# A hybrid encoder block on one NeuronCore: the input normalised ahead of its first products, decays summed by one scan per head pair

## The chip, the cores and the metric

The kernel runs on one NeuronCore of a Trainium2 chip. The metric is the device time of one execution in microseconds, lower is better; the median of several runs is compared.

## What is computed

One residual block over 512 tokens of width 1024, all in float32. The parts that matter here:

```python
h = rmsnorm(x, attn_norm_g)                     # x * rsqrt(mean(x*x) + eps) * g
proj = h @ w_in
p_sb, p_rw, p_gate = jnp.split(proj, [SB_COLS, SB_COLS + RW_COLS], axis=-1)
...
xs = token_shift(p_rw, rwkv_shift_mu)           # p + (prev - p) * mu
r, k, v, w_lo, a_lo, g_lo = jnp.split(xs, offs, axis=-1)
w_log = -jax.nn.softplus(-(decay_base + jnp.tanh(w_lo) @ decay_up)) - 0.5
decay = jnp.exp(-jnp.exp(w_log))
...
y = rwkv7_recurrence(rh, wh, kh, vh, -kk, kk * ah)
...
gates = jax.nn.sigmoid(p_gate.reshape(...) + branch_gate_b)
x = x + jnp.sum(gates * up, axis=2) @ w_out
h2 = rmsnorm(x, ffn_norm_g)
u_gate, u_val = jnp.split(causal_depthwise_conv(h2 @ w_ffn_up, ...), 2, axis=-1)
x = x + (jax.nn.silu(u_gate) * u_val) @ w_ffn_down
```

Two branches use the projection: a stick-breaking attention (8 heads) and an RWKV-7 recurrence (8 heads). The recurrence is computed in chunks of 64 tokens, and needs, in each chunk, the sum of the log decays from a token to the chunk's end.

## The kernel before

Everything is held transposed: channels on the 128 partitions, the 512 tokens along the row. A float32 product is made of three: each operand is split into a rounded high part and the rest, and high by high, high by low and low by high are summed in PSUM (`mm1`, L124). Weights come in blocks of 128 columns (`load_w`, L99): one load on SyncE's queue into `wraw`, a cast to `whi` on ScalarE, two subtractions that give the halves of `wlo` (L116), on GpSimd in the middle part of the program and on VectorE elsewhere. `wraw` and `whi` have two buffers, `wlo` three. One block of the projection is 24 products of 512 columns.

The head (L197 to L285) loads x in eight slices `xt`, scales each by the gain alone, splits it into `hhi` and `hlo`, and multiplies slices as they arrive with the first weight block w0 (the low-rank inputs of decay and iclr, bank `pl0`). The squares are summed on the side; one product with a matrix of -1 (L254) sums them over channels, and two ScalarE steps make `rs`, one factor for each token. The second block w1 (the first k of the recurrence, bank `pk0`) follows. Since the factor is missing in the products, every evacuation of a projection block multiplies by `rs` on VectorE: `evac_rw` (L362, tile u), `evac_at` (L371, tiles rawq, rawk, vT), `evac_gl` (L380, L383), `evac_gate` (L803, tile gs), and L965 late in the program.

The middle part runs three kinds of streams interleaved: four head pairs of the recurrence (`rw_stream`), four of the attention (`att_stream`), and `dense_stream`, which makes the remaining projection blocks one after the other in two PSUM banks `pd`. `interleave` (L881) orders TensorE's work by a table of latencies LAT; a scheduler orders the other engines. In `rw_stream`, the low-rank products (L410, L412) give the log decays s, a scan for each of the eight chunks sums them from the chunk's end (L425), L427 takes s off again, sll and slh (L438, L121) feed the sums over a head, and later, a solve of 31 short steps on VectorE (L538, L540) follows on transfers `sc` and `N` through DRAM. Thirteen of sixteen gate blocks are made in this part and parked in DRAM, three are made later (L962 to L966). Then come the branch products, `w_out` and the feed-forward part, with products back to back.

Of the kernel before, what the change touches and what calls it, by code (L numbers as in the profile page):

```python
# [8 lines left out]
F32 = mybir.dt.float32  # L9
F32R = mybir.dt.float32r  # L10
# [6 lines left out]
P = 128  # L17
# [35 lines left out]
def hybrid_block(ctx: ExitStack, tc: tile.TileContext, xT, w_in, vecs, decay_up, iclr_up, out_gate_up,  # L53
# [24 lines left out]
    def f(ap):  # L78
        return ap.bitcast(F32)
# [31 lines left out]
    def load_w2(w, nk=KT):  # L111
        hi, los, raw = w
        k0 = 4 * len(los)
        n = min(4, nk - k0)
        lo = wpool.tile([P, 4, P], F32R, tag="wlo", name="wlo", bufs=3)
        (G if state.get("pool") else V).tensor_tensor(lo[:, 0:n], raw[:, k0 : k0 + n], f(hi[:, k0 : k0 + n]),  # L116
                                                      op=ALU.subtract)
        los.append(lo)
# [16 lines left out]
    def bank(pool=None, tag="pd"):  # L135
        return (pool or psd).tile([P, T], F32, tag=tag, name=tag)
# [47 lines left out]
    U1 = cpool.tile([P, NC, CH // 2], F32, name="U1")  # L184

    RW0 = SBC
    LR0 = RW0 + 3 * BW
    rs = keep.tile([P, T], F32, tag="rs", name="rs")  # L190
    ph1 = ExitStack()
    psr = ph1.enter_context(tc.tile_pool(name="psr", bufs=3, space=PSUM))
    psz = ph1.enter_context(tc.tile_pool(name="psz", bufs=2, space=PSUM))
# [1 line left out]
    with tc.tile_pool(name="p0", bufs=1) as p0, \  # L195
# [8 lines left out]
        def wdma(w, c0, k0, k1):  # L204
            nc.sync.dma_start(w[2][:, k0:k1], w_in[k0 * P : k1 * P, c0 : c0 + P].rearrange("(k p) c -> p k c", p=P))

        w0, w1 = wtiles(), wtiles()
        A.dma_start(vec, vecs[:, 0:NVEC1])
        nc.sync.dma_start(xt[:, 0:1], xv[:, 0:1])
        wdma(w0, LR0, 0, 4)  # L210
        nc.sync.dma_start(xt[:, 1:2], xv[:, 1:2])
        wdma(w0, LR0, 4, 8)
        for k in range(2, KT, 2):
            nc.sync.dma_start(xt[:, k : k + 2], xv[:, k : k + 2])
        wdma(w1, RW0 + BW, 0, 8)
        lraw = [p0.tile([P, BW], F32, name=f"lraw{j}") for j in range(2)]
        for j, src in enumerate((decay_up, iclr_up)):
# [2 lines left out]
        tmpc = p0.tile([P, P], F32, name="tmpc")  # L220
        V.memset(tmpc, -1.0)
        V.tensor_copy(none_, tmpc)
        pl0, pn, pk0 = bank(psr, "pr"), bank(psr, "pr"), bank()
        sq = []
        for k in range(KT):
            if True:
                if k % 4 == 0:
                    A.copy(w0[0][:, k : k + 4], w0[2][:, k : k + 4])
                    load_w2(w0)
                act(hhi[:, k], xt[:, k], AF.Identity, scale=vcol("ag", k))  # L230
                V.scalar_tensor_tensor(hlo[:, k], xt[:, k], vcol("ag", k), f(hhi[:, k]),
                                       op0=ALU.mult, op1=ALU.subtract)
                mm1(pl0, w0, k, h_acts[k], k == 0, k == KT - 1)

                sq.append(p0.tile([P, T], F32, name=f"sq{k}"))
                if k in (0, 3):
                    G.tensor_tensor(sq[k], xt[:, k], xt[:, k], op=ALU.mult)
                else:
                    act(sq[k], xt[:, k], AF.Square)
                if 0 < k < 4:  # L240
                    G.tensor_tensor(sq[0], sq[0], sq[k], op=ALU.add)
                elif k > 4:
                    V.tensor_tensor(sq[4], sq[4], sq[k], op=ALU.add)
            if k == KT - 1:
                V.tensor_tensor(sq[0], sq[0], sq[4], op=ALU.add)
                state["pool"] = True
                for h in range(2):
                    A.copy(w1[0][:, 4 * h : 4 * h + 4], w1[2][:, 4 * h : 4 * h + 4])
                    load_w2(w1)
        for k in range(KT):  # L250
            for part in range(2):
                PE.matmul(pk0, w1[0][:, k], h_acts[k][part], start=(k + part == 0), stop=False)
            if k == 1:
                PE.matmul(pn, f(none_), sq[0], start=True, stop=True)  # L254
        for k in range(KT):
            PE.matmul(pk0, w1[1][k // 4][:, k % 4], hhi[:, k], start=False, stop=(k == KT - 1))
# [5 lines left out]
        V.tensor_scalar(ka1, vcol("keya", 0, 4), -1.0, 1.0, op0=ALU.mult, op1=ALU.add)  # L262
        qg8 = cpool.tile([P, 1], F32, name="qg8")
        V.tensor_scalar(qg8, vcol("qg"), 0.125, None, op0=ALU.mult)
        act(rs, pn, AF.Ln, scale=-1.0 / D, bias=eps_n)
        act(rs, rs, AF.Exp, scale=-0.5)
        wfirst = load_w(w_in[:, RW0 : RW0 + P], KT)
        V.tensor_tensor(sq[1], pl0, rs, op=ALU.mult)
        wal = p0.tile([P, T], F32, name="wal")
        shift_evac(wal, sq[1], 12)  # L270
        load_set(SET_SG, (AF.Sigmoid, AF.Tanh))
        act(wal[0:64], wal[0:64], AF.Tanh)
        for j in range(2):
# [15 lines left out]
        ntri = cpool.tile([P, P], F32R, name="ntri")  # L289
        idb = cpool.tile([P, P], BF16, name="idb")  # L290
        mskb = cpool.tile([P, P], BF16, name="mskb")
        one = cpool.tile([P, CH], F32, name="one")
        eps_g = cpool.tile([P, 1], F32, name="eps_g")
        V.memset(eps_g, GN_EPS)
        G.memset(ident, 0.0)
# [62 lines left out]
    AD = [dict() for _ in range(4)]  # L358

    def evac_rw(p, which, ps):  # L360
        u = rwp.tile([P, T], F32, tag="u", name="u")
        V.tensor_tensor(u, ps, rs, op=ALU.mult)  # L362
        RD[p][which] = rwp.tile([P, T], F32, tag="x" + which, name="x" + which)
        shift_evac(RD[p][which], u, 4 * "rkv".index(which) + p)

    def evac_at(p, which, ps):
        if which == "v":
            t_ = atp.tile([P, T], F32, tag="e", name="vT", bufs=3)
        else:
            t_ = atp.tile([P, T], F32, tag="raw" + which, name="raw" + which)  # L370
        V.tensor_tensor(t_, ps, rs, op=ALU.mult)  # L371
        AD[p][which] = t_

    def evac_gl(g, ps):

        u = rwp.tile([P, T], F32, tag="u", name="u")
        n = 32 if g is gl1 else P
        g_ = u[0:n]
        if n == P:
            V.tensor_tensor(g_, ps, rs, op=ALU.mult)  # L380
        else:
            A.copy(g_, ps[n : 2 * n])
            V.tensor_tensor(g_, g_, ps[0:n], op=ALU.add)  # L383
            V.tensor_tensor(g_, g_, rs[0:n], op=ALU.mult)
        y = atp.tile([P, T], F32, tag="gs", name="gy")[0:n]
        shift_evac(y, g_, 13 if n == P else 14, slice(0, n))
        act(g_, y, AF.Abs)
        act(g_, g_, AF.Exp, scale=-1.0)
        act(g_, g_, AF.Ln, bias=1.0)
        V.scalar_tensor_tensor(y, y, 0.0, g_, op0=ALU.min, op1=ALU.subtract)  # L390
        if n == P:
            his, lo = gl0[0:1], gl0[1]
        else:
            his, lo = (gl1[0:32], gl1[32:64]), gl1[64:96]
        for hi in his:
            act(hi, y, AF.Exp)
        act(g_, y, AF.Exp)
        V.tensor_tensor(lo, g_, f(his[0]), op=ALU.subtract)

    def rw_stream(p):  # L400
# [20 lines left out]
        s, ic = sic  # L421

        c = tmp(0)
        for ch in range(NC):
            V.tensor_tensor_scan(c3(c)[:, ch, ::-1], one, c3(s)[:, ch, ::-1], 0.0, op0=ALU.mult, op1=ALU.add)  # L425
        fx = tmp(1)
        V.tensor_tensor(fx, c, s, op=ALU.subtract)  # L427
        GC = rwp.tile([P, NC, 1], F32, tag="GC", name="GC", bufs=3)
# [371 lines left out]

    def evac_gate(c, b, ps):
        g = atp.tile([P, T], F32, tag="gs", name="gs", bufs=1)
        V.tensor_tensor(g, ps, rs, op=ALU.mult)  # L803
        gd = gdram.tile([P, T], F32, name=f"gd{c}_{b}")
        A.dma_start(gd, g)
        gates[c, b] = gd
# [148 lines left out]
    for c in sorted(range(KT), key=lambda c: (c, 0) in gates):  # L955
        terms = []
        for b in range(2):
            g = p2.tile([P, T], F32, tag="g", name="g", bufs=5)
            if (c, b) in gates:
                nc.sync.dma_start(g, gates[c, b])  # L960
            else:
                w = load_w(w_in[:, GOFF + b * D + c * P : GOFF + b * D + (c + 1) * P], KT)  # L962
                pg = bank(psf, "pf")
                mm3(pg, w, h_acts)
                V.tensor_tensor(g, pg, rs, op=ALU.mult)  # L965
            act(g, g, AF.Sigmoid, bias=vcol("bg", b * KT + c))  # L966
# [115 lines left out]
```

## Time and profile before

| | before |
|---|---|
| median of 3 runs | 920.23 us (919.76 to 923.12) |
| profiled execution | 921.83 us, span of its instructions 920.1 us |
| TensorE busy | 873.9 us (95% of the span) |
| VectorE busy | 625.9 us (68%) |
| ScalarE busy | 455.8 us (50%) |
| GpSimd busy | 200.2 us (22%) |
| mean granted clock of TensorE | 0.977 |

A busy TensorE is not one at its peak: its products overlap each other in the records, and they last longer at a low clock. The busy shares are means over stages that differ, so the profile is read by stretches. In the rows, PE is TensorE, PEld its weight load, DVE VectorE, ACT ScalarE, POOL GpSimd, SP SyncE; L12 is line 12 of the kernel; tile names are the program's.

### The profile page before, as it was taken

What the parts mean: (1) busy time and instruction counts of PE and PEld (TensorE: products, weight loads), DVE (VectorE), ACT (ScalarE), POOL (GpSimd) and SP (SyncE); (2) the same over time, 40 slices, a digit from 0 to 9 for tenths busy, and PEclk for the clock granted to TensorE, in tenths of its full rate; (3) what the DMA queues carried; (4) which work ended last, traced back from release to release, by engine and by line L of the source; (5) the groups of instructions that cost most, each with busy time, mean ns of one, the idle gap of its engine ahead of it and who ended that gap; (6) DMA issues with size and microseconds to landing.
All of it is one profiled execution on the core that took longest, in us unless ns stands there. A gap on an engine that the chain in (4) does not pass through costs nothing.

```text
span 920.1 us, 12850 instructions
## 1 busy us (share of the span) xinstructions
PE 873.9 (95%) x4716; PEld 675.8 (73%) x4716; DVE 625.9 (68%) x1160; ACT 455.8 (50%) x791; POOL 200.2 (22%) x219
## 2 busy tenths in 40 slices
PE   6979887898999999999999999999999999999998
PEld 3757665666767766777777888888888888888886
DVE  7585898898799679365766656777777777632322
ACT  5846665653764666358654445444444444311111
POOL 6552455326525443424000000000000000000000
PEclk9995998998999999999999999999999999999999
DMA  6320313313303331622555443333333333333331
GB/s 188 109 62 13 86 46 64 87 46 79 102 28 75 84 83 36 154 59 59 195 167 155 139 126 91 104 103 92 92 99 107 92 92 93 105 105 118 106 114 46
DMA packets 164479, 87.54 MB, mean 95 GB/s; under 512 B 28384, under 2 KB 155488, under 8 KB 164416
## 3 DMA queue, kind: packets, MB, share of 16 engines
q1 hardware_dynamic: 161392, 81.61, 31.5%
q10 hardware_dynamic: 3024, 5.11, 1.5%
q8 instruction: 37, 0.61, 0.3%
q14 instruction: 26, 0.21, 0.1%
HBM read 78.31 MB, written 8.39 MB: 94 GB/s over the span
## 4 chain that ended last, share of the span: by engine, by line
PE 71%; DVE 17%; ACT 5%; issue 3%; DMA 3%; POOL 0%; SPq 0%; ACTq 0%; DVEq 0%; POOLq 0%
PE pf L129 16%; PE pf L127 16%; PE pf L128 16%; PE pd L127 5%; PE pd L129 4%; PE pd L128 4%; DVE tm L538 3%; DVE U L540 3%; PE pr L507 2%; DMA g<-gd 1%; DVE spl L122 1%; PE pr L502 1%; ACT e L69 1%; ACT whi L105 1%; DVE wtl L754 1%
## 5 line engine op out<-in xcount | busy, mean ns | idle before, releaser
L105 ACT CAST whi<-wraw 128x1024 fp32r<-128x1024 f32 (+1 forms) x132 | 129.9, 985 | 182.6 <-PE pf L128 148.2
L116 DVE TENSOR_TENSOR wlo<-wraw,whi 128x512 fp32r<-128x512 f32 x176 | 119.0, 677 | 90.9 <-ACT whi L105 58.9
L127 PE MATMUL pf<-h2h,whi 128*128 128x512 f32 x352 | 137.3, 390 | 0.0
L128 PE MATMUL pf<-h2l,whi 128*128 128x512 f32 x352 | 136.9, 389 | 0.0
L129 PE MATMUL pf<-h2h,wlo 128*128 128x512 f32 x352 | 136.9, 389 | 0.0
L116 POOL TENSOR_TENSOR wlo<-wraw,whi 128x512 fp32r<-128x512 f32 x76 | 105.6, 1393 | 136.5 <-ACT whi L105 89.1
L127 PE MATMUL pd<-hhi,whi 128*128 128x512 f32 x296 | 128.0, 432 | 1.5 <-DVE u L380 1.5
L129 PE MATMUL pd<-hhi,wlo 128*128 128x512 f32 x296 | 121.1, 409 | 0.5 <-POOL wlo L116 0.5
L128 PE MATMUL pd<-hlo,whi 128*128 128x512 f32 x296 | 120.5, 407 | 0.0
L128 PEld LDWEIGHTS pf<-h2l,whi 128*128 128x128 f32 x352 | 66.1, 188 | 14.0 <-issue 0.2
L127 PEld LDWEIGHTS pf<-h2h,whi 128*128 128x128 f32 x352 | 66.1, 188 | 13.9 <-issue 0.2
L129 PEld LDWEIGHTS pf<-h2h,wlo 128*128 128x128 f32 x352 | 66.1, 188 | 13.6
L127 PEld LDWEIGHTS pd<-hhi,whi 128*128 128x128 f32 x296 | 57.5, 194 | 16.1 <-ACT slh L121 2.0
L129 PE MATMUL pf<-dh,wlo 128*128 128x512 f32 x176 | 69.3, 394 | 0.0
L127 PE MATMUL pf<-dh,whi 128*128 128x512 f32 x176 | 69.3, 394 | 0.0
L128 PE MATMUL pf<-dl,whi 128*128 128x512 f32 x176 | 69.3, 394 | 0.0
L129 PEld LDWEIGHTS pd<-hhi,wlo 128*128 128x128 f32 x296 | 57.6, 195 | 14.3 <-POOL wlo L116 0.9
L128 PEld LDWEIGHTS pd<-hlo,whi 128*128 128x128 f32 x296 | 57.6, 195 | 9.8 <-issue 0.2
L1021 DVE TENSOR_TENSOR u<-pf,rs 128x512 f32<-128x512 f32 x44 | 30.3, 688 | 33.4 <-PE pf L129 32.7
L121 ACT CAST dh<-cv 128x512 fp32r<-128x512 f32 x22 | 13.6, 620 | 61.8 <-DVE cv L1030 61.8
L538 DVE TENSOR_TENSOR tm<-U,N 128x60 f32<-128x60 f32 (+24 forms) x124 | 42.1, 340 | 1.9
L540 DVE TENSOR_TENSOR U<-U,tm 128x60 f32<-128x60 f32 (+24 forms) x124 | 39.6, 319 | 1.7
(306 smaller groups left out, 1665.8 us busy)
## 6 DMA issues: line engine op xcount, KB each, us to landing
wraw<-in_w_up SPq DMA_DIRECT2D x44, 512.0 KB, 3.7
wraw<-in_w_in SPq DMA_DIRECT2D x41, 512.0 KB, 3.8
wraw<-in_w_down SPq DMA_DIRECT2D x16, 512.0 KB, 4.1
wraw<-in_w_branch SPq DMA_DIRECT2D x16, 256.0 KB, 3.0
wraw<-in_w_out SPq DMA_DIRECT2D x8, 512.0 KB, 4.1
gd<-gs ACTq DMA_DIRECT2D x13, 256.0 KB, 2.0
g<-gd SPq DMA_DIRECT2D x13, 256.0 KB, 2.7
wraw<-in_w_down SPq DMA_DIRECT2D x8, 384.0 KB, 3.4
```

The lines of the kernel that those rows point to most:

```text
L69: ins = A.activation(o, i, func, **kw)
L105: A.copy(hi[:, 0:nk], raw[:, 0:nk])
L116: (G if state.get("pool") else V).tensor_tensor(lo[:, 0:n], raw[:, k0 : k0 + n], f(hi[:, k0 : k0 + n]), op=ALU.subtract)
L121: A.copy(hi, src)
L122: V.tensor_tensor(lo, src, f(hi), op=ALU.subtract)
L127: PE.matmul(ps, hi, ah, start=first, stop=False)
L128: PE.matmul(ps, hi, al, start=False, stop=False)
L129: PE.matmul(ps, lo, ah, start=False, stop=last)
L507: PE.matmul(pp[h][:, j * P : (j + 1) * P], BK[hr, ch].rearrange("p s t -> p (s t)"), ARV[hr, ch, 0 : 2 + h : 1 + h], start=True, stop=True)
L538: V.tensor_tensor(tv, U[:, 0:m, q : q + 1].broadcast_to([P, m, n]), N[:, q : q + 1, q + 1 :].broadcast_to([P, m, n]), op=ALU.mult)
L540: V.tensor_tensor(U[:, 0:m, q + 1 :], U[:, 0:m, q + 1 :], tv, op=ALU.add)
L1021: V.tensor_tensor(u, ps, rs2, op=ALU.mult)
```

## The change

The head now forms the factor first. All of x is loaded ahead of the weights; the squares go pairwise through four products with the matrix of -1; `rs` is written to a PSUM bank; each slice is multiplied by gain and factor (`xn`), split, and multiplied with w0 and w1 side by side. So no evacuation multiplies by `rs` any more: the recurrence's inputs are shifted straight from PSUM, the attention's and the gates' are copied by ScalarE, the late gates' sigmoid reads PSUM. The eight scans become one over 512 columns, with a factor row `one` that is 0 where a chunk begins. `wlo` gets a fourth buffer, and the scratch that is set aside for DMA descriptors is made smaller.

```diff
-        lo = wpool.tile([P, 4, P], F32R, tag="wlo", name="wlo", bufs=3)
+        lo = wpool.tile([P, 4, P], F32R, tag="wlo", name="wlo", bufs=4)
...
-    rs = keep.tile([P, T], F32, tag="rs", name="rs")
...
-        nc.sync.dma_start(xt[:, 0:1], xv[:, 0:1])
-        wdma(w0, LR0, 0, 4)
-        nc.sync.dma_start(xt[:, 1:2], xv[:, 1:2])
-        wdma(w0, LR0, 4, 8)
-        for k in range(2, KT, 2):
-            nc.sync.dma_start(xt[:, k : k + 2], xv[:, k : k + 2])
+        for k0, k1 in ((0, 1), (1, 2), (2, 4), (4, 6), (6, 7), (7, 8)):
+            nc.sync.dma_start(xt[:, k0:k1], xv[:, k0:k1])
+        wdma(w0, LR0, 0, 8)
         wdma(w1, RW0 + BW, 0, 8)
...
-                act(hhi[:, k], xt[:, k], AF.Identity, scale=vcol("ag", k))
-                V.scalar_tensor_tensor(hlo[:, k], xt[:, k], vcol("ag", k), f(hhi[:, k]),
-                                       op0=ALU.mult, op1=ALU.subtract)
-                mm1(pl0, w0, k, h_acts[k], k == 0, k == KT - 1)
...
+        for k in range(0, KT, 2):
+            sq = [p0.tile([P, T], F32, tag=f"sq{j}", name=f"sq{j}", bufs=2) for j in range(2)]
+            for j in range(2):
+                act(sq[j], xt[:, k + j], AF.Square)
+            V.tensor_tensor(sq[0], sq[0], sq[1], op=ALU.add)
+            PE.matmul(pn, f(none_), sq[0], start=(k == 0), stop=(k == KT - 2))
+        act(rs, pn, AF.Ln, scale=-1.0 / D, bias=eps_n)
+        act(rs, rs, AF.Exp, scale=-0.5)
+        for w in (w0, w1):
+            for h in range(2):
+                A.copy(w[0][:, 4 * h : 4 * h + 4], w[2][:, 4 * h : 4 * h + 4])
+                load_w2(w)
+
         for k in range(KT):
+            xn = p0.tile([P, T], F32, tag="xn", name="xn", bufs=3)
+            V.scalar_tensor_tensor(xn, xt[:, k], vcol("ag", k), rs, op0=ALU.mult, op1=ALU.mult)
+            A.copy(hhi[:, k], xn)
+            (V if k % 2 else G).tensor_tensor(hlo[:, k], xn, f(hhi[:, k]), op=ALU.subtract)
+            for ps, w in (pl0, w0), (pk0, w1):
+                PE.matmul(ps, w[0][:, k], hhi[:, k], start=(k == 0), stop=False)
+                PE.matmul(ps, w[1][k // 4][:, k % 4], hhi[:, k], start=False, stop=False)
+            for ps, w in (pl0, w0), (pk0, w1):
+                PE.matmul(ps, w[0][:, k], hlo[:, k], start=False, stop=(k == KT - 1))
...
-        V.tensor_tensor(sq[1], pl0, rs, op=ALU.mult)
         wal = p0.tile([P, T], F32, name="wal")
-        shift_evac(wal, sq[1], 12)
+        shift_evac(wal, pl0, 12)
...
-        one = cpool.tile([P, CH], F32, name="one")
+        one = cpool.tile([P, T], F32, name="one")
...
         V.memset(one, 1.0)
+        V.memset(one[:, 0:T:CH], 0.0)
...
     def evac_rw(p, which, ps):
-        u = rwp.tile([P, T], F32, tag="u", name="u")
-        V.tensor_tensor(u, ps, rs, op=ALU.mult)
         RD[p][which] = rwp.tile([P, T], F32, tag="x" + which, name="x" + which)
-        shift_evac(RD[p][which], u, 4 * "rkv".index(which) + p)
+        shift_evac(RD[p][which], ps, 4 * "rkv".index(which) + p)
...
-        V.tensor_tensor(t_, ps, rs, op=ALU.mult)
+        A.copy(t_, ps)
         AD[p][which] = t_
...
-        for ch in range(NC):
-            V.tensor_tensor_scan(c3(c)[:, ch, ::-1], one, c3(s)[:, ch, ::-1], 0.0, op0=ALU.mult, op1=ALU.add)
+        V.tensor_tensor_scan(c[:, ::-1], one, s[:, ::-1], 0.0, op0=ALU.mult, op1=ALU.add)
...
         g = atp.tile([P, T], F32, tag="gs", name="gs", bufs=1)
-        V.tensor_tensor(g, ps, rs, op=ALU.mult)
+        A.copy(g, ps)
...
-                V.tensor_tensor(g, pg, rs, op=ALU.mult)
-            act(g, g, AF.Sigmoid, bias=vcol("bg", b * KT + c))
+                act(g, pg, AF.Sigmoid, bias=vcol("bg", b * KT + c))
...
-    nc = bacc.Bacc("TRN2", target_bir_lowering=False, num_devices=1)
+    nc = bacc.Bacc("TRN2", target_bir_lowering=False, num_devices=1, dynamic_dma_scratch_size=1024)
```

ScalarE's queue in the head, from the weight casts to the first use of the factor (`whi` casts of L248 are w1's; `rs` is the factor). Before:

```order
L248 CAST whi<-wraw 128x512 x2
L282 CAST lt<-lraw_125 128x512
L284 CAST lup_78<-lraw_125 64x512
L284 CAST lup_79<-lraw_126 64x512
L282 CAST lt<-lraw_126 128x512
L69 ACTIVATE rs<-pr,eps_n 128x512
L105 CAST whi<-wraw 128x1024
L69 ACTIVATE rs<-rs 128x512
L63 ACT_TABLE_LOAD
L69 ACTIVATE wal<-sq_152,mu_237 128x512
```

Now, with the factor in the bank `pz`:

```order
L230 CAST whi<-wraw 128x512 x2
L69 ACTIVATE pz<-pr,eps_n 128x512
L230 CAST whi<-wraw 128x512
L69 ACTIVATE pz<-pz 128x512
L230 CAST whi<-wraw 128x512
L63 ACT_TABLE_LOAD
L236 CAST hhi<-xn 128x512
```

Between the two steps that make the factor stands a cast of w1, and between the factor and the first `hhi` another cast and the table load. Before, `hhi` did not wait for the factor.

VectorE's queue in the decay chain of pair 0 (`sll` feeds a product that TensorE waits for). Before:

```order
L164 SCALAR_TENSOR_TENSOR xr<-u,vec,xr 128x511
L417 SCALAR_TENSOR_TENSOR t_356<-pr,ndb,t_356 128x512
L425 SCALAR_TENSOR_TENSOR t_396<-one,t_356 128x64 x8
L362 TENSOR_TENSOR u<-pd,rs 128x512
L427 TENSOR_TENSOR t_405<-t_396,t_356 128x512
L417 SCALAR_TENSOR_TENSOR t_390<-pr,ndb,t_390 128x512
L164 SCALAR_TENSOR_TENSOR xv<-u,vec,xv 128x511
L438 TENSOR_TENSOR sll<-t_356,slh 128x512
```

Now:

```order
L164 SCALAR_TENSOR_TENSOR xr<-pd,vec,xr 128x511
L397 SCALAR_TENSOR_TENSOR t_370<-pr,ndb,t_370 128x512
L404 SCALAR_TENSOR_TENSOR t_408<-one,t_370 128x512
L397 SCALAR_TENSOR_TENSOR t_402<-pr,ndb,t_402 128x512
L406 TENSOR_TENSOR t_410<-t_408,t_370 128x512
L417 TENSOR_TENSOR sll<-t_370,slh 128x512
L164 SCALAR_TENSOR_TENSOR xv<-pd,vec,xv 128x511
```

Eight scans have become one (it is printed as SCALAR_TENSOR_TENSOR like the step before it), the product u is gone, and the shift of xv stands behind sll instead of ahead of it.

SyncE's queue at the transfers of pair 0's solve (`sc` takes blocks out, `N` brings them back in the solve's layout). Before:

```order
L520 DMA sc<-QA 32x4x32 x8
L103 DMA wraw<-in_w_in 128x8x128
L531 DMA N<-sc 32x1024 x4
```

Now:

```order
L499 DMA sc<-QA 32x4x32 x4
L103 DMA wraw<-in_w_in 128x8x128
L499 DMA sc<-QA 32x4x32 x4
L510 DMA N<-sc 32x1024 x4
```

A weight load has moved from behind the eight transfers to between their halves.

## Rows read from the trace of the kernel before

**Rows 1.** Busy time by stretch: PE, PEld, DVE, ACT, POOL, granted clock, DMA.
```profile
28.80:445.00 416.20, 382.43 (x2625) 280.81 (x2624) 321.90 (x701) 249.52 (x522) 183.50 (x196) 0.95 0.27 71
445.00:920.00 475.00, 471.04 (x2045) 382.44 (x2043) 284.09 (x424) 188.15 (x243) 0.00 (x0) 1.00 0.37 112
68.50:89.00 20.50, 20.50 (x81) 14.01 (x82) 11.34 (x26) 10.87 (x20) 4.30 (x6) 0.50 0.09 22
218.00:226.00 8.00, 6.23 (x25) 5.09 (x27) 5.85 (x11) 2.43 (x5) 2.99 (x2) 0.57 0.40 111
```

**Rows 2.** TensorE's waits, 28 to 458 us: total us, times, longest.
```profile
PE pz L748 <- DVE spl L122: 4.2, 7, 1.2
PE pr L700 <- DVE vT L371: 4.1, 1, 4.1
PE pr L150 <- ACT slh L121: 4.0, 1, 4.0
...
PE pr L151 <- DVE sll L438: 2.8, 1, 2.8
...
PE pd L127 <- DVE u L380: 1.5, 1, 1.5
```

**Rows 3.** Timeline of 20 to 30 us: start, duration, engine, line, instruction.
```profile
21.75 0.63 PE L252 MATMUL pd<-hlo,whi 128*128 128x512 f32 x1
...
23.04 1.55 PE L254 MATMUL pr<-sq,none 128*128 128x512 f32 x2
...
25.21 1.04 ACT L105 CAST whi<-wraw 128x1024 fp32r<-128x1024 f32 x1
...
26.79 1.28 ACT L63 ACT_TABLE_LOAD   x1
...
27.19 1.98 PE L256 MATMUL pd<-hhi,wlo 128*128 128x512 f32 x8
...
28.40 2.99 POOL L116 TENSOR_TENSOR wlo<-wraw,whi 128x512 fp32r<-128x512 f32 x2 [0.79 <-PE pd L256]
...
28.84 1.40 DVE L164 SCALAR_TENSOR_TENSOR wal<-sq,vec,wal 128x511 f32<-128x511 f32 x1 [1.35 <-ACT wal L69]
```

**Rows 4.** Instructions on tile xt: duration ns min/median/max, first and last start us.
```profile
L69 ACT ACTIVATE hhi<-xt,vec x8: 705/708/721, 5.1 to 14.2; 128x512 fp32r<-128x512 f32 x8
L231 DVE SCALAR_TENSOR_TENSOR hlo<-xt,vec,hhi x8: 736/768/1795, 5.8 to 18.5; 128x512 fp32r<-128x512 f32 x8
L69 ACT ACTIVATE sq<-xt x6: 612/614/615, 6.3 to 14.8; 128x512 f32<-128x512 f32 x6
L214 SPq DMA_DIRECT2D xt<-in_xT x3: 469/469/507, 2.7 to 3.8; - x3
...
DMA to landing us min/median/max: 2.8/5.4/7.9
```

**Rows 5.** Chain of waits, 28 to 75 us: start, us, what.
```profile
42.52 1.25 issue
43.76 2.41 DVE t L425 x7
...
48.91 0.66 DVE xv L164
...
67.06 0.63 ACT slh L121
```

**Rows 6.** Groups of instructions, 28 to 458 us: busy, mean ns | idle before, releaser.
```profile
L425 DVE TENSOR_TENSOR_SCAN t<-one,t 128x64 f32<-128x64 f32 x32 | 12.1, 432 | 2.1 <-ACT t L69 2.1
...
L803 DVE TENSOR_TENSOR gs<-pd,rs 128x512 f32<-128x512 f32 x13 | 8.9, 687 | 6.6 <-DMA gd<-gs 4.9 <-PE pd L129 1.6
L362 DVE TENSOR_TENSOR u<-pd,rs 128x512 f32<-128x512 f32 x12 | 8.2, 681 | 1.7 <-PE pd L129 1.7
...
L371 DVE TENSOR_TENSOR rawq<-pd,rs 128x512 f32<-128x512 f32 x4 | 2.8, 690 | 5.0 <-PE pd L129 5.0
```

**Rows 7.** GpSimd's wait for a free wlo buffer, whole span.
```profile
POOL wlo L116 <- PE pd L129: 44.0, 24, 6.2
```

More of the change, by code (lines that the diff above doesn't have):

```diff
@@ L222, in hybrid_block @@
         V.tensor_copy(none_, tmpc)
-        pl0, pn, pk0 = bank(psr, "pr"), bank(psr, "pr"), bank()
-        sq = []
-        for k in range(KT):
[L226 to L229, printed above, removed]
-                act(hhi[:, k], xt[:, k], AF.Identity, scale=vcol("ag", k))
-                V.scalar_tensor_tensor(hlo[:, k], xt[:, k], vcol("ag", k), f(hhi[:, k]),
-                                       op0=ALU.mult, op1=ALU.subtract)
-                mm1(pl0, w0, k, h_acts[k], k == 0, k == KT - 1)
[L235 to L256, printed above, removed]
+        pl0, pn, pk0, rs = bank(psr, "pr"), bank(psr, "pr"), bank(), bank(psz, "pz")
+        for k in range(0, KT, 2):
[4 more added lines that the diff above has]
+            PE.matmul(pn, f(none_), sq[0], start=(k == 0), stop=(k == KT - 2))
@@ L257, in hybrid_block @@
+        state["pool"] = True
         mu1 = cpool.tile([P, 15], F32, name="mu1")
@@ L264, in hybrid_block @@
         V.tensor_scalar(qg8, vcol("qg"), 0.125, None, op0=ALU.mult)
-        act(rs, pn, AF.Ln, scale=-1.0 / D, bias=eps_n)
-        act(rs, rs, AF.Exp, scale=-0.5)
         wfirst = load_w(w_in[:, RW0 : RW0 + P], KT)
-        V.tensor_tensor(sq[1], pl0, rs, op=ALU.mult)
         wal = p0.tile([P, T], F32, name="wal")
-        shift_evac(wal, sq[1], 12)
+        shift_evac(wal, pl0, 12)
         load_set(SET_SG, (AF.Sigmoid, AF.Tanh))
@@ L378, in evac_gl @@
         g_ = u[0:n]
-        if n == P:
-            V.tensor_tensor(g_, ps, rs, op=ALU.mult)
-        else:
+        if n < P:
             A.copy(g_, ps[n : 2 * n])
             V.tensor_tensor(g_, g_, ps[0:n], op=ALU.add)
-            V.tensor_tensor(g_, g_, rs[0:n], op=ALU.mult)
         y = atp.tile([P, T], F32, tag="gs", name="gy")[0:n]
-        shift_evac(y, g_, 13 if n == P else 14, slice(0, n))
+        shift_evac(y, ps if n == P else g_, 13 if n == P else 14, slice(0, n))
         act(g_, y, AF.Abs)
@@ L960, in hybrid_block @@
                 nc.sync.dma_start(g, gates[c, b])
+                act(g, g, AF.Sigmoid, bias=vcol("bg", b * KT + c))
             else:
```

## The prediction

> **What bounds the kernel now.** I read the busy time by stretch first. From 28.8 to 445 us (normalisation done, the 512-token branches running) TensorE is busy 382 of 416 us and VectorE 322 of 416, so neither is saturated throughout; from 445 us to the end TensorE is busy 471 of 475 us [rows 1]. The second stretch is bound by products alone, and the change takes none away there: what it is worth must come out of the 445 us before. Next, TensorE's waits between 28 and 458 us. The reader is to see that the long ones end on VectorE, or on ScalarE just behind VectorE: 4.1 us for vT, 4.0 for slh, 2.8 for sll, 1.5 for a PSUM bank that u (L380) empties, 4.2 in seven pieces for spl [rows 2]. Then the clock: 68.5 to 89 us ran wholly at 0.50 of full speed, the lower level of 1.2 GHz, right behind the wait for slh; 218 to 226 us had a mean of 0.57, around the wait for vT [rows 1, 2]. So an idle TensorE costs twice: the wait, and slower products behind it. Last, the chain of waits before slh: it runs through the short scans and the shift of xv, and ends at slh at 67.7 us [rows 5].
>
> The profiled execution took 921.83 us, 1.6 above the median of the three runs (920.23). I form a difference against it and take that from the median. About 0.5%, or 4.6 us, is what a measurement of this kernel can tell from no change.
>
> **Removed from VectorE.** Twelve u (8.2 us), twelve of the q, k, v evacuations (12 x 0.69 = 8.3), thirteen gs (8.9), two steps in evac_gl (0.7 each, as gs: 1.4) [rows 6]. The 32 short scans take 12.1 us together; four long ones stand in their place [rows 6]. No row shows a 512-wide scan: at least an elementwise step of that width, 0.69, at most eight short ones at their undisturbed pace. The seven in the chain took 2.41 with the first of them disturbed, so eight cost at most 2.8 [rows 5, 6]. I take 1.2, nearer the lower end, because most of a 64-wide step is not its 64 elements; 12.1 - 4.8 = 7.3 saved. Sum 34 of VectorE's 322 us, about a tenth.
>
> **Added to ScalarE.** Twelve q, k, v copies and thirteen gate copies at 0.61 (a square of the same size) [rows 4]: 15.3 us on an engine with 250 of 416 us busy [rows 1]. Between nothing and all 15.3 could lie on the path; I take a tenth, +1.5. The three gates after 445 us lose a VectorE product beside a busy TensorE: nothing, the products hide it; if that cover went, it would be 0.7 each.
>
> **The head, slower.** Before, x and w0 shared the queue and the last x landed 3.8 + 7.9 = 11.7 us in [rows 4]. Now 2.0 of those 2.5 MB go ahead: by bytes 9.5, and I take 10.0. Then two squares (1.2), one VectorE sum (0.7), a four-pass product (1.55), the logarithm (0.7), a weight cast that ScalarE's order puts ahead of the exponential (0.6), the exponential (0.6), another cast (0.6), a table load (1.28), the cast of hhi (0.6) [rows 3, 4, 6]: 17.8, with hand-overs 18.3. There the first of 48 products starts, where the kernel before was in the midst of them. Early products are slow: one lasted 0.63 at 21.75 us; the eight at 27.19 follow each other by (1.98 - 0.4)/7 = 0.23 [rows 3], so 0.45 at half speed. Between none of them slow (end 29.3) and all (39.9) I take nine, since they run without a hole, and the eight at 27.19 had got fast behind such a run: 9 take 4.1 and 39 take 8.9, end 31.3, against 27.19 + 1.98 = 29.2 [rows 3]. VectorE supplies a slice in about 1.1 (0.74 and half of 0.69), six fast products take 1.38: no limit [rows 3, 4, 6]. But w0's buffer is read to the end now, so the next block's cast (1.04) and low part (2.99/2 = 1.5) start only at 31.0 [rows 3]: its products run freely from 33.5, TensorE is **4 us late**. The decay chain: cast 1.04, shift 0.71, VectorE 0.74: wal at 33.5, against 28.84 + 1.40 = 30.2, **3.3 late** [rows 3, 4].
>
> Here a rule of the skill enters. That wal took 1.40 while GpSimd's wlo ran from 28.40 for 2.99 us [rows 3]; now its source lies in PSUM, and I count the 0.74 that the quickest of its kind take on hlo [rows 4]. The Trainium skill, SBUF — State Buffer, section "SBUF: two separate sides", says that a VectorE instruction with two SBUF inputs and a GpSimd instruction lock each other out of a shared port pair. By that rule a PSUM source escapes it, and so does xn; were it not so, the head would be 0.66 later.
>
> **Pair 0's chain.** Behind wal fall away: scans 2.41 and their disturbed beginning of about 1.3, less 1.2 for the new one; a u (0.68) behind the scans; and xv (0.66), which the new order puts behind sll: 3.8 for sll. Further a rawq and a rawk of 0.69 each in the queue ahead of slh [rows 5, 6]: 5.2 in all. Slh, done at 67.06 + 0.63 = 67.7, comes 3.3 - 5.2 = -1.9, say **-1.8**. TensorE's 4 us of lateness are swallowed by its own waits of 2.8 and 4.0 on just this chain [rows 2].
>
> **Behind it.** (a) The wait before 68.5 us shrinks and with it the slow stretch: at most half of 20.5 = 10.3 us could come back [rows 1], at least nothing; I take -2, since some wait remains and the stretch is made of many short products. (b) Waits: vT becomes a ScalarE copy that no longer stands in VectorE's queue, -3 of 4.1; the u of L380 goes, -1 of 1.5; a tenth less VectorE work shortens the others, -1.5: together -5.5, bounds 0 and the whole of 4.1 + 1.5 + 4.2 = -9.8 [rows 2]. (c) The slow piece at 218: 86% of 8 us at half level, at most -3.4, I take -1.5 [rows 1].
>
> Two things at nothing. The shifted evacuations hold a PSUM bank longer (0.71 and 0.74 instead of 0.68 [rows 4, 6]); the bank is wanted two blocks later, and one block is 24 x 0.23 = 5.4 us, which hides it. If a bank were late each time, twelve would add 9 us. SyncE's order moves a weight load between two halves of the sc transfers; it waits there for a buffer whose release hangs on GpSimd's wlo. Those wait 44.0 us for TensorE now [rows 7], and the fourth wlo buffer loosens just that. A load that still waits delays N and with it the solve.
>
> **Sum:** -1.8 - 2 - 5.5 - 1.5 + 1.5 = **-9.3**: 912.5 for the profiled execution, **911 us** for the median.
>
> **The rivals.**
> 1. *Absorbed.* The order of TensorE is fixed, so a wait removed reappears at the next late thing: the solve's short VectorE steps, a late N, GpSimd's products. Then the head's loss and pair 0's gain stay (-1.8), (a) and (c) don't come, (b) gives a third: -1.8 - 1.8 + 1.5 = -2.1, 918 us. For it: most of VectorE's chain is work that stays. Against: VectorE's queue is shared by all of it, and gets a tenth shorter.
> 2. *ScalarE becomes the queue: slower.* It runs in order; a copy that has come to its head before TensorE is done with the block stops the exponentials and casts behind it. VectorE's evacuations wait for TensorE today, rawq 5.0 us in all, gs 6.6 with its DMA, u 1.7 [rows 6]: 13.3 us, moving over with 15.3 of work. If half of these 28.6 us comes onto the path, +14.3, and (b) stays out: -1.8 - 2 - 1.5 + 14.3 = +9.0, 929 us. It decides where more than about 10 us (the rest of the sum) get onto the path. For it: the wait of gs for its buffer now stands before all of ScalarE's work. Against: ScalarE is idle 40% of this stretch [rows 1].
> 3. *The clock stays low in the head.* The four norm products stand alone, and nothing runs while the scale is formed, so the 48 begin at the low level. If they all stay there: 18.3 + 48 x 0.45 = 39.9 instead of 31.3. The decay chain hangs on the last of them, so the 8.6 us reach slh undiminished: -9.3 + 8.6 = -0.7, so 919.5 us. The Trainium skill, TensorE: Matmul & The Clock Gate, section "HAM oscillation", warns that idle gaps put the engine back to the low clock, which speaks against an order that gathers the products behind the norm; that agrees with the slow stretch at 68.5.
> 4. *All slow stretches go*, (a) whole: -9.3 - 8.3 = -17.6, 903 us. It needs the wait for slh to vanish.
>
> **How the numbers follow.** Forecast 0.45, absorbed 0.19, ScalarE 0.13, low clock 0.08, all slow stretches gone 0.15. The predicted time is the forecast's, 911. The range runs from 900, a little below rival 4, to 923; outside lie rival 2 and a tail below. Faster by over 0.5% (under 915.6): 0.45 + 0.15 = 0.60. Within: 0.19 + 0.08 = 0.27. Slower: 0.13.
>
> **What would show it.** First of the 48 products near 18 us and the last near 31; a long scan of about 1.2; slh near 66; the wait for vT mostly gone; the low clock behind slh shorter than 20 us; VectorE some 34 us less busy, ScalarE some 15 more; the stretch from the first gate after the branches as long as before (475 us). I am wrong if TensorE has new waits on ScalarE copies of more than a few us, or if the head costs more than 4.

## The result

The changed kernel takes **917.16 us** (median of 12 runs, 911.22 to 921.63), the kernel before 923.09 (12 runs beside it, 919.76 to 924.53): ratio 0.9941 [0.992, 0.9963], or -5.4 us [-7.4, -3.4]. It is faster, by a little over the 0.5% named above; forecast was 1.0%, -9.3 us. The time lies in the range, the size does not come out. (The 911 us were taken from a median of 920.23; from the 923.09 measured here the same difference would have given 913.8.) The profiled execution took 918.29 us, 1.1 above its median. Medians and ranges in this document take in every execution; the ratios leave out three near 937 us, in experiments 4 and 6, whose mean granted clock was 0.954 to 0.956.

Below, two rows of busy time by stretch (columns as in [rows 1]), then the slow stretch that answers to 68.5 to 89.

```profile
28.80:445.00 416.20, 384.50 (x2652) 282.82 (x2651) 288.40 (x638) 262.72 (x549) 185.29 (x197) 0.97 0.27 71
445.00:916.50 471.50, 467.81 (x2035) 380.98 (x2034) 275.72 (x419) 187.74 (x241) 0.00 (x0) 1.00 0.37 113
72.90:83.10 10.20, 9.78 (x43) 7.20 (x42) 5.35 (x9) 6.47 (x13) 0.05 (x1) 0.50 0.21 56
```

VectorE lost 321.9 - 288.4 = 33.5 us between 28.8 and 445, ScalarE gained 13.2, as the sum had it (34 and 15). The stretch at the low level behind slh is half as long, 10.2 us for 20.5. TensorE's waits between 28 and 458 us (columns as in [rows 2]):

```profile
PE pz L727 <- DVE spl L122: 4.7, 7, 1.4
...
PE pr L150 <- ACT slh L121: 2.5, 1, 2.5
PE pr L390 <- DVE rkb L465: 2.2, 1, 2.2
PE pr L151 <- DVE sll L622: 1.9, 1, 1.9
PE pd L127 <- ACT whi L105: 1.8, 2, 0.9
...
PE pd L129 <- POOL wlo L116: 1.5, 3, 0.7
```

The wait of 4.1 us for vT is gone; those for spl are as long as before; waits for weights (whi, wlo) are new but for 0.5 us. The groups of instructions (as [rows 6]) have the long scan at 1.24 us a piece, and ScalarE's copies of the gates with 1.4 us of waiting ahead of all thirteen:

```profile
L404 DVE TENSOR_TENSOR_SCAN t<-one,t 128x512 f32<-128x512 f32 x4 | 5.0, 1241 | 2.5 <-ACT t L69 2.5
...
L782 ACT COPY gs<-pd 128x512 f32<-128x512 f32 x13 | 7.6, 585 | 1.4 <-PE pd L129 1.3
```

The head, in rows of the timeline (as [rows 3]):

```profile
15.02 0.66 ACT L69 ACTIVATE pz<-pr,eps_n 128x512 f32<-128x512 f32 x1 [1.82 <-PE pr L225]
15.60 0.61 ACT L230 CAST whi<-wraw 128x512 fp32r<-128x512 f32 x1
16.11 0.59 ACT L69 ACTIVATE pz<-pz 128x512 f32<-128x512 f32 x1
...
17.24 1.28 ACT L63 ACT_TABLE_LOAD   x1
...
19.20 0.79 PE L239 MATMUL pr<-hhi,whi 128*128 128x512 f32 x1 [4.23 <-ACT hhi L236]
...
32.74 0.39 PE L242 MATMUL pd<-hlo,whi 128*128 128x512 f32 x1
32.94 1.04 ACT L105 CAST whi<-wraw 128x1024 fp32r<-128x1024 f32 x1 [4.75 <-PE pr L242]
...
34.06 5.47 POOL L116 TENSOR_TENSOR wlo<-wraw,whi 128x512 fp32r<-128x512 f32 x4 [5.99 <-ACT whi L105]
...
34.61 0.75 DVE L164 SCALAR_TENSOR_TENSOR wal<-pr,vec,wal 128x511 f32<-128x511 f32 x1 [4.79 <-ACT wal L69]
...
36.71 3.36 DVE L260 TENSOR_TENSOR wl<-wal,wl 64x512 fp32r<-64x512 f32 x2 [1.35 <-ACT wl L259]
```

The first of the 48 products starts at 19.2 (18.3 predicted), the last at 32.7 and ends at 33.1 (31.3); TensorE was at the low level from 18.3 to 25.1 us, which took in fourteen products, not nine. wal is done at 35.4, not 33.5. GpSimd then makes four low parts in one go.

Where the time went is read best from one chain: the start of pair 0's first scan, the end of slh (L121), the first transfer N of pair 0, the start of its solve, the first gate product behind the branches, the end of the span. All from timelines, in us, with the low-clock stretch near 70 us; four kernels of the experiments stand beside. Each row is one execution, and executions of one kernel differ (last section), so a row shows how that execution went.

| | scan | slh | N | solve | gate | end | low clock |
|---|---|---|---|---|---|---|---|
| before | 42.5 | 67.7 | 92.5 | 100.1 | 445.4 | 920.1 | 20.5 |
| after | 48.5 | 71.4 | 95.5 | 104.3 | 443.2 | 916.5 | 10.2 |
| scan alone | 42.7 | 66.4 | 86.6 | 93.2 | 439.1 | 914.1 | 6.8 |
| after, three buffers | 46.9 | 69.8 | 88.3 | 95.9 | 436.3 | 909.6 | 6.8 |
| after, two order rules | 48.1 | 69.3 | 89.1 | 97.2 | 436.6 | 909.9 | 6.8 |
| three buffers, short scans | 48.3 | 73.4 | 97.6 | 106.3 | 443.0 | 916.7 | 10.2 |

After the change pair 0 is late all the way: scan +6.0, slh +3.7, solve +4.2. The solve itself makes this good, 43.2 us for 48.1; VectorE does 41.0 us of work in it for 46.4, six instructions fewer:

```profile
100.10:148.20 48.10, 40.80 (x189) 29.54 (x187) 46.37 (x103) 28.14 (x57) 27.78 (x23) 0.96 0.18 51
```
```profile
104.30:147.50 43.20, 35.63 (x151) 25.38 (x151) 40.96 (x97) 25.85 (x52) 23.69 (x22) 0.96 0.17 47
```

(The first row is of before, the second of after; columns as in [rows 1].) VectorE is busy 41.0 of 43.2 us there, so the solve is still VectorE's.

### The profile page after: what moved, and what is told of

It reads as the page before. It is cut to its first block, busy times and chain, and to the rows that moved or that the text cites. A ratio compares the mean times of both kernels' runs of the same rounds, so it can differ in the third digit from the quotient of the medians.

```text
span 916.5 us, 12769 instructions
## 1 busy us (share of the span) xinstructions
PE 869.6 (95%) x4722; PEld 673.6 (73%) x4722; DVE 581.5 (63%) x1096; ACT 468.2 (51%) x818; POOL 194.0 (21%) x216
## 4 chain that ended last, share of the span: by engine, by line
PE 64%; DVE 5%; ACT 2%; issue 1%; POOL 1%; DVEq 0%; ACTq 0%; POOLq 0%
PE pf L127 17%; PE pf L128 17%; PE pf L129 17%; PE pd L127 3%; PE pd L129 2%; PE pd L128 2%; DVE U L519 1%; DVE tm L517 1%; ACT e L69 1%; DVE spl L122 1%; POOL wlo L116 0%; PE pr L587 0%; DVE wtl L733 0%; PE pz L694 0%; PE pz L727 0%
## 5 line engine op out<-in xcount | busy, mean ns | idle before, releaser
L116 DVE TENSOR_TENSOR wlo<-wraw,whi 128x512 fp32r<-128x512 f32 (+1 forms) x178 | 113.7, 676 | 81.8 <-ACT whi L105 79.6
L116 POOL TENSOR_TENSOR wlo<-wraw,whi 128x512 fp32r<-128x512 f32 x74 | 101.4, 1391 | 120.0 <-ACT whi L105 105.5
L129 PEld LDWEIGHTS pf<-h2h,wlo 128*128 128x128 f32 x352 | 66.1, 188 | 13.7
L129 PE MATMUL pf<-dh,wlo 128*128 128x512 f32 x176 | 69.3, 394 | 0.0
L127 PE MATMUL pf<-dh,whi 128*128 128x512 f32 x176 | 69.3, 394 | 0.0
L128 PE MATMUL pf<-dl,whi 128*128 128x512 f32 x176 | 69.3, 394 | 0.0
L121 ACT CAST dh<-cv 128x512 fp32r<-128x512 f32 x22 | 13.7, 621 | 62.0 <-DVE cv L1009 62.0
L519 DVE TENSOR_TENSOR U<-U,tm 128x60 f32<-128x60 f32 (+24 forms) x124 | 43.3, 350 | 2.0
L129 PEld LDWEIGHTS pf<-dh,wlo 128*128 128x128 f32 x176 | 32.9, 187 | 8.3
```

The lines of the kernel that those rows point to most:

```text
L121: A.copy(hi, src)
L127: PE.matmul(ps, hi, ah, start=first, stop=False)
L128: PE.matmul(ps, hi, al, start=False, stop=False)
L129: PE.matmul(ps, lo, ah, start=False, stop=last)
L519: V.tensor_tensor(U[:, 0:m, q + 1 :], U[:, 0:m, q + 1 :], tv, op=ALU.add)
```

## The experiments

Differences in us are the ratio less 1, times the median of before in the same comparison; their 95% intervals stand in brackets.

**1. The scan alone.** The kernel before, with one scan per pair and the smaller scratch.

```diff
-        for ch in range(NC):
-            V.tensor_tensor_scan(c3(c)[:, ch, ::-1], one, c3(s)[:, ch, ::-1], 0.0, op0=ALU.mult, op1=ALU.add)
+        V.tensor_tensor_scan(c[:, ::-1], one, s[:, ::-1], 0.0, op0=ALU.mult, op1=ALU.add)
```

> The kernel before with the scan alone changed (and the small DMA scratch, which makes room for its longer row of ones). Theory A (the gain of the change comes from a lighter VectorE, the head eats most of it): the long scans take 1.3 us each instead of 12.1 us for the 32 short ones, VectorE about 7 us less busy between 28.8 and 445 us, sll of pair 0 about 1.3 us earlier than at 50.2 us; time 1 to 2 us below the kernel before (ratio 0.998 to 0.999). Theory B (TensorE's fixed order absorbs what VectorE saves): no difference to the kernel before, ratio 1.000 within 0.002, although VectorE is as much less busy.

915.43 us (913.55 to 916.24), **-8.9 [-10.6, -7.2]**: this part alone gives more than the whole change. slh comes only 1.3 us earlier, but the low-clock stretch behind it is 6.8 us instead of 20.5, and N is issued 5.9 us earlier (table). The edit changed more than VectorE, though: TensorE's order behind slh is another one, too. Pair 0's inner products (those that the masks and `sc` wait for) stood in fours behind the first group of eight, before:

```profile
69.45 1.17 PE L507 MATMUL pr<-ARV,BK 64*128 64x128 f32 x8
...
73.63 1.16 PE L507 MATMUL pr<-ARV,BK 64*128 64x128 f32 x4
...
77.21 1.16 PE L507 MATMUL pr<-ARV,BK 64*128 64x128 f32 x4
```

With the scan alone the next groups are of eight, too:

```profile
69.11 1.17 PE L507 MATMUL pr<-ARV,BK 64*128 64x128 f32 x8
...
74.05 0.68 PE L507 MATMUL pr<-ARV,BK 64*128 64x128 f32 x8
...
76.59 0.67 PE L507 MATMUL pr<-ARV,BK 64*128 64x128 f32 x8
```

The same split runs through all the traces. Where the second group is of eight (experiments 1, 2, 5, 7, 9, 10 and the second of 8), the low-clock stretch near 70 us lasts 3.4 to 10.2 us; where it is of four (before, after, experiments 3, 4, 6 and the first of 8), 10.2 to 23.9. No run separates the shorter scan from the order that came with it.

**2. The change with three wlo buffers.**

```diff
-        lo = wpool.tile([P, 4, P], F32R, tag="wlo", name="wlo", bufs=4)
+        lo = wpool.tile([P, 4, P], F32R, tag="wlo", name="wlo", bufs=3)
```

> The changed kernel with three wlo buffers instead of four. Theory A: the fourth buffer is of little weight, time within 2 us of the changed kernel's 917; in the head GpSimd can no longer make four low halves in a row from 34 us, so the low-rank chain (second part of wl) is done about 1 us earlier and the second dense block about 1 us later. Theory C (the fourth buffer lets GpSimd run ahead and lock VectorE out, and that is where the gain went): 3 us or more below the changed kernel, under 914.

912.95 (911.33 to 914.34), **-11.3 [-13.1, -9.4]**. The fourth buffer costs nearly 6 us, on the medians of these runs. At the highest clocks the two kernels are level: with four buffers 911.22 and 911.93 us at a mean granted clock of 0.989, with three 911.33 and 911.46 at 0.991. Lower down they are not: 918.29 at 0.981 with four, 912.95 at 0.981 with three. So the cost comes in some executions and not in others. The buffer does what the prediction said to GpSimd's waits (all of the span; total, times, longest). After:

```profile
POOL wlo L116 <- ACT whi L105: 105.5, 22, 11.2
```

With three buffers:

```profile
POOL wlo L116 <- ACT whi L105: 89.7, 24, 8.4
POOL wlo L116 <- PE pd L129: 38.7, 19, 6.0
```

The wait for TensorE (44.0 before, [rows 7]) is gone with four; and still the kernel is slower.

**3. The 25 copies back on VectorE**, from PSUM, without the product by rs.

```diff
-        A.copy(t_, ps)
+        V.tensor_copy(t_, ps)
...
-        A.copy(g, ps)
+        V.tensor_copy(g, ps)
```

> The changed kernel with the 25 copies of q, k, v and gates back on VectorE (as plain copies out of PSUM, without a factor). Theory A: ScalarE is no bottleneck and VectorE's load counts, so 1 to 4 us above the changed kernel's 917 (918 to 921), with VectorE 17 us busier from 28.8 to 445 us. Theory D (ScalarE's queue holds up the chain): faster than the changed kernel, 914 or less.

919.92 (911.36 to 922.36), -4.5 [-6.7, -2.4], against -5.4 for the change: no difference that can be told. A queue on ScalarE that holds up the chain would have shown as a gain here; there is none.

**4. Three whi buffers**, so that the next block's cast need not wait for w0.

```diff
-        hi = wpool.tile([P, KT, P], F32R, tag="whi", name="whi")
+        hi = wpool.tile([P, KT, P], F32R, tag="whi", name="whi", bufs=3)
```

(in all three places where whi is made)

> The changed kernel with three whi buffers instead of two, so that the first dense block's high parts can be cast while w0 and w1 are still being read. Theory A: TensorE starts the first dense block right behind the 48 products near 33 us and runs it without holes, instead of 34.0 and freely only from 35.4; the shift of wal no longer stands behind that cast on ScalarE, so wal is done near 34.3 instead of 35.4; pair 0's slh comes 1 to 2 us earlier than 71.4; time 1 to 3 us below the changed kernel's 917. Theory B (TensorE's order absorbs): the first dense block starts as much earlier, but the time stays at 917 within 1 us.

919.66 (917.61 to 937.14), -3.4 [-5.3, -1.5]. The second low-rank product of pair 0 (L392) starts at 36.4 us instead of 40.1, yet the median does not come earlier. The trace is of an execution of 925.37 us, 5.7 above the median; in it the low clock lasts 23.9 us from 67.7. One more buffer again brought an earlier start and no gain.

**5. Four buffers, TensorE's order as with three.** Two order rules (no wait on data) for pair 0: slh's squares product ahead of the 39th dense product, not behind the 48th; the last inner products (L486) ahead of the 128th, not behind the 135th.

```diff
+    tc.add_manual_dep(DN[38].ins, FX["slh"].ins.name, _ORDER, reason="slh ahead")
+    tc.add_manual_dep(DN[127].ins, FX["st1"].ins.name, _ORDER, reason="inner products ahead")
```

> The changed kernel with its four remainder buffers, but with two order rules added for pair 0: the first squares product of the normalisation of the keys (slh) stands ahead of the 39th product of the dense blocks instead of behind the 48th, and the last inner products of step one stand ahead of the 128th instead of behind the 135th. By this TensorE's order becomes that of the kernel with three buffers (4 of 4135 rows differ, before 60), while GpSimd still may make four remainders ahead and SyncE still puts a weight load between the halves of the scratch transfers. Theory O (the fourth buffer costs by the order that it lets the scheduler fix on TensorE): as the three-buffer kernel, 912 to 914.5 us, pair 0's inverse starting at 95 to 98 us of the trace and not at 104. Theory G (it costs because GpSimd runs four remainders ahead and holds VectorE and its own later work up, or because of the weight load on SyncE): 916 to 918 us, the inverse starting at 102 or later.

911.83 (909.96 to 918.38), **-10.5 [-13.1, -7.9]**, the solve starting at 97.2: theory O. Its interval and that of the change (-5.4 [-7.4, -3.4]) just fail to touch. GpSimd still runs ahead, SyncE still has the weight load between the halves of sc, and neither costs what was lost. VectorE's timeline shows what went with the order. After:

```profile
83.41 0.42 DVE L489 TENSOR_TENSOR QA<-pr,maskq 128x256 f32<-128x256 f32 x1 [2.32 <-PE pr L486]
...
84.97 0.42 DVE L489 TENSOR_TENSOR QA<-pr,maskq 128x256 f32<-128x256 f32 x1 [0.69 <-PE pr L486]
85.31 1.22 DVE L404 TENSOR_TENSOR_SCAN t<-one,t 128x512 f32<-128x512 f32 x1
...
88.74 0.74 DVE L489 TENSOR_TENSOR QA<-pr,maskq 128x256 f32<-128x256 f32 x2
...
93.12 0.42 DVE L489 TENSOR_TENSOR QA<-pr,maskq 128x256 f32<-128x256 f32 x1
```

With the two rules:

```profile
79.77 0.76 DVE L495 TENSOR_TENSOR QA<-pr,maskq 128x256 f32<-128x256 f32 x2 [2.55 <-PE pr L490]
...
82.17 1.49 DVE L406 TENSOR_TENSOR_SCAN t<-one,t 128x512 f32<-128x512 f32 x1
83.59 0.72 DVE L495 TENSOR_TENSOR QA<-pr,maskq 128x256 f32<-128x256 f32 x2
...
85.49 0.41 DVE L495 TENSOR_TENSOR QA<-pr,maskq 128x256 f32<-128x256 f32 x1
...
86.75 0.43 DVE L495 TENSOR_TENSOR QA<-pr,maskq 128x256 f32<-128x256 f32 x1 [0.16 <-PE pr L490]
```

Of the eight masks that sc waits for, six come singly in the first and the last at 93.1; in the second six come in pairs and the last at 86.8. Pair 1's scan and three other steps stand among them in both. N follows at 95.5 and 89.1.

**6. The fourth buffer in the kernel before**, with the smaller scratch.

> The kernel before with the fourth remainder buffer and the smaller scratch, and nothing else. Theory O (the cost is in the order that comes with it): here the order on TensorE moves little (27 of 4132 rows, the first squares product of pair 0 two products later), so the time stays within 1.5 us of the kernel before, 921 to 924. Theory G (GpSimd running ahead costs by itself): 5 to 6 us slower, 927 to 929. What the prediction said of the buffer (harmless, or a small gain where a load waited): 920 to 923.

927.51 (922.70 to 937.21), +4.6 [1.9, 7.4]: worse than theory O had it, near the lower end of G's. Pair 0 isn't slower here (its solve runs from 99.6 to 147.1); the later pairs are, whose solves take 45.2, 33.2 and 34.9 us where before had 41.9, 31.8 and 32.5. That the buffer costs without this change too is shown; whether by the order of pair 1's steps, which also moved, is not separated. So theory O, which experiment 5 bears out in the changed kernel, did not foretell this one.

**7. Three buffers and the eight short scans**: the head and the freed evacuations without the scan.

> The three-buffer version of the changed kernel with the eight short scans per pair put back, so the new head and the 25 removed VectorE products alone. If the parts add: the kernel before less what is left of the three-buffer kernel's 11 us when the scan's 8.8 us are taken off, 919 to 921. If both parts only end the same slow stretch of TensorE in pair 0, so that either suffices: 913 to 916. If the late head costs more than the evacuations give as long as the scans stay: 922 or more.

918.37 (916.62 to 919.54), **-5.0 [-6.5, -3.6]**. With the scan's -8.9 that would be 13.9, and together they give 11.3: they add but for 2.6, which the three intervals do not tell from nothing. Both have a shorter slow stretch than before (6.8 and 10.2 us for 20.5).

**8. One rule of the two.** First the last inner products early, slh late; then the opposite, with these products held behind the 135th.

> The changed kernel, four buffers, with one of the two order rules: the last inner products of pair 0's step one stand at the 123rd product of the dense blocks and not at the 135th; the first squares product (slh) stays late, behind the 48th. If the place of the last inner products is what costs (theory L): 912 to 914 us, the inverse of pair 0 starting at 96 to 99 us of the trace. If the late slh costs (theory S): 916 to 918, starting at 102 or later.

> The changed kernel, four buffers, with the opposite half: slh early, behind the 38th product of the dense blocks, and the last inner products held behind the 135th, as the changed kernel has them. Theory L: 916 to 918 us, the inverse of pair 0 starting at 102 us or later. Theory S: 912 to 914, starting at 96 to 99.

The first: 913.66 (910.42 to 916.66), -9.7 [-12.3, -7.2]; the second: 915.94 (913.61 to 919.71), -6.9 [-9.3, -4.4]. The medians lean to theory L, but the intervals overlap, and the second's is not told from the change's -5.4. The traces bear theory L out in the second, where the solve starts at 103.9, and not in the first, where it starts at 104.4. There the last inner products were placed earlier, and yet the transposes that lead them ran at 92.0 (91.7 after the change); they waited for a bank:

```profile
92.03 0.27 PE L485 MATMUL pr<-ident,BK 64*128 64x64 f32 x1 [0.40 <-ACT QA L499]
```

In this trace pair 1's solve took 33.9 us for 39.7 (40.0 with both rules). So neither place alone starts the solve early; both rules together do. What each does inside step one is not separated further: the early slh brings the eights of experiment 1 and a low-clock stretch of 6.8 us, the early inner products alone leave the fours and 10.2 us.

**9. The scan for pair 0 alone**, in the kernel before.

> The kernel before with one scan for pair 0 alone and eight short ones for pairs 1 to 3. If the scan's gain of 8.8 us comes from pair 0's chain, whose end lets the slow stretch of TensorE end and the first inverse start 7 us earlier: 914 to 917 us. If each pair gives its 2 us: 920 to 922.

916.14 (914.89 to 918.61), -6.8 [-8.8, -4.8], so by the medians about three quarters of the scan's -8.9 come from pair 0 (the intervals overlap); 2 us a pair it is not. Its stretch from 64 to 84 us ran at a mean granted clock of 0.83, as with all four scans; before at 0.61:

```profile
64.00:84.00 20.00, 16.27 (x63) 10.79 (x63) 10.71 (x18) 8.87 (x16) 5.01 (x7) 0.61 0.12 30
```
```profile
64.00:84.00 20.00, 16.65 (x99) 11.01 (x99) 16.65 (x29) 13.21 (x25) 8.87 (x9) 0.83 0.13 31
```

(First before, then this kernel: 63 and 99 TensorE instructions, not all of one size, in 16.3 and 16.7 busy us.)

**10. ScalarE's order in the head mended**, with three buffers, and with four and the two rules.

```diff
+                if w is w1:
+                    tc.add_manual_dep(ci.ins, ex.ins.name, _ORDER, reason="casts of w1 behind the factor")
...
-        load_set(SET_SG, (AF.Sigmoid, AF.Tanh))
+        load_set(SET_SG, (AF.Sigmoid, AF.Tanh), behind=[ch_.ins])
```

(ci is a cast of the weights, ex the Exp of the factor, ch_ the last cast of hhi)

> The three-buffer version of the changed kernel with ScalarE's order in the head mended: the casts of the second weight block behind the Exp of the factor, and the load of the sigmoid table behind the last cast of the activations. The first of the 48 products should come 1 to 2 us earlier (17 to 18 us of the trace, not 19.2). If the head's lateness counts one for one: 911 to 912 us. If TensorE's fixed order absorbs it: 912 to 914, no difference from the three-buffer kernel.

> The changed kernel, four buffers, with both order rules and the mended head (casts of the second block behind the Exp, table load behind the last cast). If order and head add as they do with three buffers: 908 to 911 us, the lowest of this study; if four buffers eat the head's part: 911 to 913.

**909.85** (909.01 to 911.02), -13.4 [-15.0, -11.7], and **910.65** (909.31 to 911.23), -12.9 [-15.2, -10.6]: the two lowest of the study, and faster than both kernels. In the first, the 48 products start at 17.08 us instead of 18.77 with three buffers alone, the last of them 2.8 us earlier:

```profile
17.08 0.80 PE L243 MATMUL pr<-hhi,whi 128*128 128x512 f32 x1 [2.92 <-ACT hhi L240]
...
29.54 0.39 PE L246 MATMUL pd<-hlo,whi 128*128 128x512 f32 x1
```

N follows 1.8 us earlier. The median is 3.1 us lower, 2.1 by the ratios: by the medians the head's lateness is paid nearly in full. The intervals overlap, as do those with and without the mended head on top of the two rules (-12.9 and -10.5), so how much of it is paid is not certain.

## Why the prediction was wrong in size

**The step that failed is "Two things at nothing", in its second half**: "the fourth wlo buffer loosens just that". The wait went as said; what I counted as harmless or helpful costs 5.9 us (-5.4 with it, -11.3 without). In this kernel the order laid down with the buffer accounts for it: with four buffers and the three-buffer order on TensorE the change gives -10.5. How the order costs stays open in part: the best executions with four buffers are as fast as those with three (experiment 2), and in the kernel before the buffer costs 4.6 us with little of TensorE's order moved (experiment 6). Where a scheduler fixes the order by what it thinks is free, a buffer moves instructions on every engine, and for that the sum had no term. The SyncE order it named as the danger is there in experiment 5 as well, at no cost that can be seen.

Without that step the total of -9.3 would have been about right (-10.5 or -11.3 measured), but that is luck in part, by two sizes that were off in opposite ways:

- **The head and pair 0's chain** were too cheap. slh was to come at 65.9 and came at 71.4. The scan starts 6.0 late, not 3.3: five products more at the low level, wl behind GpSimd's four low parts, and oguh's transfer ahead of pair 0's exponential on ScalarE. From there to slh the chain takes 22.9 us for 25.2, so 2.3 of the 5.2 fell away. That "TensorE's 4 us of lateness are swallowed" by its waits no run tests alone: of the waits it named, 2.8 for sll is gone and 4.0 for slh is 2.5, with 1.2 new on the same chain, while the mended head of experiment 10 brings TensorE 2.8 us forward and pair 0's scan 2.6 with it (44.4 for 46.9).
- **The scan** was too small: 7.3 us of VectorE's time and a part of a 5.2 us gain, measured -8.9 alone. The term mis-sized most is (a), which took -2 of a bound of -10.3: the slow stretch falls from 20.5 to 6.8 us with the scan alone (half of the 13.7 us between them is 6.9), and N comes 5.9 us earlier. Its mechanism was not this one, though. The wait for slh did not shrink (3.9 us with the scan alone, 4.0 before), and rival 4 was wrong that the stretch needs that wait to vanish; what is seen to differ behind slh is TensorE's order (experiment 1), for which (a) had no term.

Right, by their rows: the long scan (1.2; measured 1.24), though not for the reason given, that most of a 64-wide step is not its 64 elements: eight short scans in a row took 1.57 us in experiment 6 (last section), hardly more than the long one; VectorE -33.5 and ScalarE +13.2; vT's wait gone; no ScalarE queue (rival 2, experiment 3); the late stretch unchanged but for 1.4 us (473.3 for 474.7). Term (c) did not come: the low-clock stretch near 220 us is 6.8 us long in both. Rival 1, absorbed, described where after ended (918 us; 917.16 measured) better than the forecast did, though for another reason: with three buffers the change gives -11.3, not rival 1's -2.1. Rival 3 came in part: fourteen low-level products, then the full level for the rest.

What the prediction took for wal came so: reading PSUM, it took 0.75 us beside GpSimd's low parts, while the two subtractions of wl, with both inputs in SBUF, took 3.36 together, and 2.37 before. The Trainium skill, SBUF — State Buffer, "SBUF: two separate sides", states that a VectorE instruction with two SBUF inputs and a GpSimd instruction that reads SBUF lock each other out of a shared port pair; these rows agree with it.

## What to carry to other kernels

A buffer that removes a wait can still cost time where a scheduler orders the engines: compare the order on all of them, and try the change without the buffer, before counting it at nothing. Price a shorter chain ahead of a slow-clock stretch by that stretch too, since 4.6 of the 5.9 us by which the scan alone brought N forward arose behind slh; and look at the order of those products, not at the wait alone. And undo a change part by part: here one part gave -8.9, one -5.0, and one took back 5.9.

## What the runs showed of the hardware

Two things were not expected. The same program ranges over 10 us from run to run with the mean granted clock: the changed kernel took 911.22 and 911.93 us at 0.989, 914.3 to 916.0 at 0.983, and 919 to 921.6 at 0.976 to 0.978; so its median says less than its interval. And a short scan is not slow by itself. Eight 64-wide scans in a row took 3.70 us in the kernel before and 4.76 in experiment 7, where GpSimd was subtracting for most of that time, but 1.57 in experiment 6, where GpSimd stood idle from 43.5 to 45.4 us. Before:

```profile
42.41 1.28 POOL L345 TENSOR_TENSOR ogu<-og__329,ogu 32x512 fp32r<-32x512 f32 x1
42.47 3.70 DVE L425 TENSOR_TENSOR_SCAN t<-one,t 128x64 f32<-128x64 f32 x8 [1.57 <-ACT t L69]
44.65 1.37 POOL L116 TENSOR_TENSOR wlo<-wraw,whi 128x512 fp32r<-128x512 f32 x1 [0.96 <-ACT whi L105]
```

Experiment 6:

```profile
41.89 1.60 POOL L345 TENSOR_TENSOR ogu<-og__329,ogu 32x512 fp32r<-32x512 f32 x1
43.81 1.57 DVE L425 TENSOR_TENSOR_SCAN t<-one,t 128x64 f32<-128x64 f32 x8 [0.79 <-ACT t L69]
45.37 3.00 POOL L116 TENSOR_TENSOR wlo<-wraw,whi 128x512 fp32r<-128x512 f32 x2 [1.89 <-issue]
```

One 512-wide scan took 1.21 to 1.32 us in the changed kernel, and 2.30 in experiment 1, where GpSimd was at work at its start. By these rows most of what one scan saves over eight is disturbance: undisturbed, eight take 0.3 us more than one.
